# A layer on one Trainium2 core: the dilated attention's mixing split over two steps and fetched back by GpSimd, the next pair's inputs loaded in parts

## The chip, the cores and the metric

The kernel runs on one of the eight cores of one Trainium2 chip. A core has five engines, each with its own instruction queue that it works off in order: TensorE (PE; its weight loads are listed as PEld), VectorE (DVE), ScalarE (ACT), GpSimd (POOL) and SyncE (SP, which here only starts transfers). Transfers can be started from the queues of SP, ACT and GpSimd. The metric is the time of one execution on the device in microseconds (us); lower is better. An engine that reaches an instruction whose inputs are not there, or whose buffer is not free, stands still, and everything behind it in its queue stands too.

## What is computed

One encoder layer on a sequence of 2048 tokens of width 1024, all in 32-bit floats. The part that matters here is the second mixer, the dilated attention of eight heads of 64. It is computed three times, with dilations 1, 4 and 16, and the three results are mixed for each token and head by their log-denominators:

```python
for window, dil in ((128, 1), (512, 4), (2048, 16)):
    half = window // (2 * dil)
    # tokens of the same residue modulo dil form one sequence of 2048 / dil
    o, lse = banded_attention(sub(q), sub(k), sub(v), bias, half, half, None)
    outs.append(o); lses.append(lse)
w = softmax(stack(lses), axis=0)
o = sum(w[..., None] * stack(outs), axis=0)
```

Before it come an RMS norm, the projections to q, k and v of both mixers, and a windowed attention; behind it an output projection with norm and residual, a large feed-forward part with norms, and a gate over a projected side input. The tolerance asks for nearly full 32-bit products, so a large product is made of three matmuls on values split into a high and a low part (`split`: ACT rounds the high part, DVE subtracts it).

## The kernel before

The layer runs in stages: projections, group a (the windowed attention), **group b** (the dilated attention), stage c (the second half of the output projection, norms and transposes), the feed-forward part, the gate. The order of the instructions on every engine is the order in which the program text issues them; there is no planner in the stages from group a on. The work is laid out by hand in steps:

- `Pipe.step` is one step of group b. An item (`b_item`) is one half of a 512-token bank of one pair of heads for one dilation `p`; it has four parts. In step t the step issues `scores` and `probs` of item t, `values` of item t - 3 and `turn` of item t - 2, then calls `feed_b`, then `tick`. There are 96 items: for each of four pairs of heads, the dilations in the order p = 2 (16), 0 (1), 1 (4), eight items each. Items of p = 2 have half as much work as the others.
- `scores` (L806) are matmuls into two buffers of the three of `ps_s`. `probs` (L819, L822) reduces them on DVE (row minimum into `tm`) and takes the exponential on ACT (row sums into `dn`). `turn` transposes on PE into `pt` (two buffers, `ps_t`) and DVE copies to `et`. `values` multiplies with `v` into `po` (one buffer), and every second item ACT evicts `po` to `ops_` (L856, L859, L861).
- `later(dt, fn)` puts a call into the `tick` of the step dt steps on; `tick` comes last in a step.
- `feed_b` first advances every running mixing by one `yield`, then lets `wo_first` go one piece on, in three steps of four from step 12 on (the fourth, t modulo 4 = 3, has none), and from step 86 on `ple`. `wo_first` is the first half of the output projection: six matmuls into `psm` to a piece, four pieces to a tile. The last piece of a tile evicts `psm` (`sgt`, L950), and splits the next tile `o` (`oh_`, `ol_`, L128 and L129, then a square on ACT and sums on GpSimd, L659 to L661); the first piece of the next tile contains the matmul `pss` (L666) on these sums and starts the load of the tile after (L653).
- `mix(pair, ...)` mixes the three results of one pair. It is started by `turn` of the pair's last item, two steps into the next pair's p = 2 items, and takes part in the step in which it starts. Its parts up to the next `yield`: (1) for the row minima and then for the row sums (`kind` 0 and 1): three transposes on PE into one `px`, three copies on ACT (L877, L879, L881), two small writes to DRAM (`sd`, L882, L884, issued by ACT), and then the two loads `sv` (L887), which bring these sums back in token order, from SP; (2) nothing; (3) `mn` and `wt` on DVE (L891 to L894) and an exponential on ACT; (4) five DVE operations, product, sums, reciprocal and the weights `wt` (L898 to L904); (5) the high part `ch` of the weights on ACT (L908, `wr` in the profile); (6) the low part `cl` on DVE (L910); then eight row blocks. A row block has four matmuls `cps` (L917) in two `ps_s` buffers, two DVE products (L920) and two sums on GpSimd (L923, L924); after every second the result goes to DRAM (`obd`, L927). For pairs 0 to 2 the yields stand after blocks 0, 1, 3, 5 and 7, for pair 3 after each.
- The next pair's inputs are loaded by SP when the buffer's last reader has been issued: q after the scores of the last p = 2 item, k with the first p = 0 item, `v` of each dilation after the values of its last item. q, k and `v` for p = 2 are one transfer of 1 MB each; `v` for p = 0 is two (of 256 and 960 KB), `v` for p = 1 is eight of 256 KB, all eight issued in one step.
- The small tiles `text` (biases, L414), `o` (L653) and others share two buffers, `raws`. A load into one of them waits on SP for its last reader, and what follows on SP waits with it.
- After the last item a closing loop advances the last mixing, with two pieces of `ple` in each pass; in its eleventh pass (`loops == 10`) it puts the loads (`c_load`, L1026) and splits (`c_split`) for stage c on the clock, and stage c starts four ticks after that or when the loop ends, whichever is later.

Of the kernel before, what the change touches and what calls it, by code (L numbers as in the profile page):

```python
# [59 lines left out]
def layer(ctx, tc, a, out):  # L60
    nc = tc.nc
    pe, act, dve, pool, sp = nc.tensor, nc.scalar, nc.vector, nc.gpsimd, nc.sync
# [18 lines left out]
    qkd = [dram.tile([128, S], F32, name=f"qkd{i}") for i in range(13)]  # L81
    vad = dram.tile([S, 128], F32, name="vad")
    vb3 = dram.tile([16, 128, 512], F32, name="vb3")
    vb1a = dram.tile([4, 128, 512], F32, name="vb1a")
    vb1o = dram.tile([15, 128, 512], F32, name="vb1o")
# [26 lines left out]
    def row_ap(v, off, ap):  # L112
        return bass.AP(tensor=v.tensor, offset=v.offset + off, ap=ap)
# [121 lines left out]
    def natural(dst, src, half, eng):  # L235
        eng(dst.rearrange("p (a r) -> p a r", r=R)[:, :, 8 * half : 8 * half + 8], src.rearrange("p (r a) -> p a r", r=8))
# [7 lines left out]
    with ExitStack() as st:  # L244
        pst = st.enter_context(tc.tile_pool(name="pst", bufs=3, space=PSUM, reuse_waits="tile"))
        psm = st.enter_context(tc.tile_pool(name="psm", bufs=5, space=PSUM, reuse_waits="tile"))
        with ExitStack() as st1:
# [27 lines left out]
            for tb in range(4):  # L275
                for n in range(4):
                    if tb == 0 and n < 3:
                        c, pl = ((VA0, w1), (0, wcp), (128, wcp))[n]
# [82 lines left out]
    vps = {2: bpre}  # L361
    kps = [bpre, None]

    def load_q(pair):
        q = bpre.tile([128, S], F32, name="bq", tag="bq")
        sp.dma_start(q, qkd[5 + pair])
        return q

    def load_k(pair):
        k = kps[pair % 2].tile([128, S], F32, name="bk", tag="bk")  # L370
        sp.dma_start(k, qkd[9 + pair])
        return k

    VROW, VCHUNK = 512, 128 * 512

# [8 lines left out]
                         row_ap(vb3, (4 + 8 * c) * VROW, [[VCHUNK, 16], [1, n]]))  # L384
            yield

    def load_v(pair, p):
        c0 = 128 * pair
        cols = slice(c0, c0 + 128)
        v = vps[p].tile([128, (19, 32, 16)[p], 128], F32, name=f"v{p}", tag=f"v{p}")  # L390
        if p == 2:
            sp.dma_start(v, vb3[:, :, cols].rearrange("c p n -> p c n"))
        elif p == 0:
            sp.dma_start(v[:, 0:4, :], vb1a[:, :, cols].rearrange("c p n -> p c n"))
            sp.dma_start(v[:, 4:19, :], vb1o[:, :, cols].rearrange("c p n -> p c n"))
        else:
            for b4 in range(4):
                for n, a0 in ((0, 0), (16, 16)):
                    m = 15 if n and b4 == 3 else 16
                    sp.dma_start(v[32 * b4 : 32 * b4 + 32, n : n + m, :],  # L400
                                 row_ap(vb3, 4 * b4 * VCHUNK + a0 * VROW + c0, [[VROW, 32], [32 * VROW, m], [1, 128]]))
        return v

    def load_b3(pair):
# [14 lines left out]
    def later(dt, fn):  # L419
        todo.setdefault(clock[0] + dt, []).append(fn)  # L420
# [64 lines left out]
    st_b = {}  # L485
# [208 lines left out]
    def load_wo_first(to):  # L694
        def part(k):
            halves = load_wo_k(*((wcp, "wc", 2) if k < 2 else (wop, f"wo{k}", 1)), k)
            later(4, lambda: to.append(halves()))

        for k, dt in enumerate((0, 0, 4, 5)):
            later(dt, lambda k=k: part(k))  # L700
# [6 lines left out]
    with ExitStack() as st:  # L707
# [50 lines left out]
        def b_item(pair, p, bank, half):  # L758
# [26 lines left out]
            def scores():  # L785
                if first_ and p == 2:
                    if pair == 0:
                        st_b["v"][0, 0] = load_v(0, 0)
                        st_b["b"][0, 0] = load_bias(0, 1, st_b["text"])
                        later(2, lambda: load_wo_first(st_b["wa"]))  # L790
                        later(10, lambda: st_b["b"].update({(0, 1): load_bias(0, 2)}))
                        later(12, lambda: st_b["v"].update({(0, 1): load_v(0, 1)}))
                        later(18, load_sel)
                    st_b["tm"] = [bp.tile([128, 32], F32, name=f"tm{i}", tag=f"tm{i}", bufs=2) for i in range(3)]
                    st_b["dn"] = [bp.tile([128, 32], F32, name=f"dn{i}", tag=f"dn{i}", bufs=2) for i in range(3)]
                    st_b["qn"] = bm.tile([128, S], F32, name="qn", tag="qn")
                    for hf in range(2):
                        natural(st_b["qn"], st_b["q"][:, hf * S // 2 : (hf + 1) * S // 2], hf, pool.tensor_copy)
                if first_ and p == 0 and pair < 3:
                    st_b["k"][pair + 1] = load_k(pair + 1)  # L800
                box.update(q=st_b["q"], qn=st_b["qn"], k=st_b["k"][pair], vt=st_b["v"][pair, p], tm=st_b["tm"], dn=st_b["dn"])
                ps = box["ps"] = [ps_s.tile([128, 512], F32, name="ps_s", tag="ps_s") for _ in range(2)]
                box["at"] = [place(2 * half + jj) for jj in range(2)]
                for jj, (lq, rk, var, vc) in enumerate(box["at"]):
                    for hh in range(2):
                        pe.matmul(ps[hh][:, 256 * jj : 256 * jj + w], lq[HH[hh]], rk[HH[hh]], start=True, stop=True)  # L806
                if last_ and p == 2 and pair < 3:
                    st_b["q"] = load_q(pair + 1)

            def probs():  # L810
                e = box["e"] = ep.tile([128, 2, 512], F32, name="e", tag="e")
# [29 lines left out]
            def values():  # L841
                if half == 0:
                    st_b["po"] = ps_o.tile([128, 512], F32, name="po", tag="po")
                po = st_b["po"]
                for jj, (lq, rk, var, vc) in enumerate(box["at"]):
                    j = 2 * half + jj
                    for c in range(nch):
                        s0 = 128 * (nch * jj + c)
                        for hh in range(2):
                            pe.matmul(po[HH[hh], 128 * j : 128 * j + 128], vc[c][:, HH[hh]],  # L850
                                      box["et"][hh][:, s0 : s0 + 128], start=c == 0, stop=c == nch - 1)
                if half == 1:
                    opt = ops_[:, op_of(pair, p)]
                    if p == 0:
                        ov = views(opt, 0)[:, :, 32 * bank : 32 * bank + 32].rearrange("p r (j a) -> p r j a", j=4)
                        act.activation(ov, po.rearrange("p (j a r) -> p r j a", j=4, r=R), AF.Copy)  # L856
                    elif p == 1:
                        ov = views(opt, 1)[:, :, bank, :].rearrange("p b (m a) -> p b m a", m=4)
                        act.activation(ov, po.rearrange("p (m a b) -> p b m a", m=4, b=4), AF.Copy)  # L859
                    else:  # L860
                        act.activation(opt[:, 512 * bank : 512 * bank + 512], po, AF.Copy)  # L861
                if last_ and pair < 3:
                    st_b["v"][pair + 1, p] = load_v(pair + 1, p)

            return scores, probs, turn, values

        def mix(pair, tms, dns):
            sd = dram.tile([4, 32, 128], F32, name=f"sd{pair}")
            sv = xp.tile([32, 2, 3, 128], F32, name="sv", tag="sv")
            lo_ = min(op_of(pair, p) for p in range(3))  # L870
            s0, s2 = 1 - lo_, op_of(pair, 2) - lo_
            for kind, srcs in enumerate((tms, dns)):
                px = ps_t.tile([32, 3, 128], F32, name="px", tag="pt")
                for p in range(3):
# [8 lines left out]
                             tr[:, 0, :].rearrange("n (r a) -> n r a", r=R))  # L883
                act.dma_start(row_ap(sd, (2 * kind + 1) * 4096, [[32, 32], [1024, 4], [1, 32]]),  # L884
                             tr[:, 1, :].rearrange("n (b a) -> n b a", b=4))
            for kind in range(2):
                sp.dma_start(sv[:, kind, s0 : s0 + 2, :], sd[2 * kind : 2 * kind + 2].rearrange("k p a -> p k a"))  # L887
            yield
            yield
            mn = xp.tile([32, 128], F32, name="mn", tag="mn")  # L890
# [13 lines left out]
            dve.tensor_mul(wt, wt, rz.unsqueeze(1).to_broadcast([32, 3, 128]))  # L904
            wr = xp.tile([32, 2, 3, 128], F32R, name="wr", tag="sv")
            ch, cl = wr[:, 0], wr[:, 1]
            yield
            act.activation(ch, wt, AF.Copy)  # L908
            yield
            dve.tensor_sub(cl, wt, ch.bitcast(F32))  # L910
# [2 lines left out]
            for n, rr in enumerate(order):  # L913
                for r in (2 * rr, 2 * rr + 1):
                    ps = ps_s.tile([128, 512], F32, name="cps", tag="ps_s")
                    for c, st_, sp_ in ((ch, True, False), (cl, False, True)):
                        pe.matmul(ps[:, 0:384], sel[:, 128 * r : 128 * r + 128], c.rearrange("n k a -> n (k a)"),  # L917
                                  start=st_, stop=sp_)
                    ov = ops_[:, lo_ : lo_ + 3, 128 * r : 128 * r + 128]
                    dve.tensor_tensor(ov, ov, ps[:, 0:384].rearrange("p (k n) -> p k n", k=3), op=ALU.mult)  # L920
                hs = slice(256 * rr, 256 * rr + 256)
                om = oms[rr // 2][:, 256 * (rr % 2) : 256 * (rr % 2) + 256]
                pool.tensor_tensor(om, ops_[:, lo_, hs], ops_[:, lo_ + 1, hs], op=ALU.add)  # L923
                pool.tensor_tensor(om, om, ops_[:, lo_ + 2, hs], op=ALU.add)  # L924
                if n % 2 == 1:
                    qt = rr // 2
                    later(2, lambda qt=qt: sp.dma_start(obd[qt][128 * pair : 128 * pair + 128, :], oms[qt]))  # L927
                if n not in (2, 4, 6) or pair == 3:
                    yield
        def wo_first():  # L930
            wa = st_b["wa"]
# [124 lines left out]
        while mixers:  # L1056
# [3 lines left out]
            if loops == 10:  # L1060
                schedule_c(4)
                start = clock[0] + 4
# [353 lines left out]
    for s in range(E_):  # L1416
        n, hf = s // 2, s % 2
# [243 lines left out]
```

## Time and profile before

| | |
|---|---|
| median of 3 runs | 2747.43 us (2746.08 to 2748.78) |
| the profiled execution | 2751.77 us |
| its span, first to last instruction | 2750.0 us |
| granted TensorE clock, mean | 0.994 |
| PE busy / DVE / ACT / GpSimd | 97% / 64% / 46% / 34% |
| transfers | 324.40 MB, 118 GB/s on average |
| group b in the span | about 590 to 1090 us |

All times of single instructions are from the one profiled execution. A row of the timeline gives the start and the duration in us, the engine, the line of the kernel, the operation, what it writes and reads, how many were merged, and in brackets the idle time of the engine just before, with the instruction or transfer that ended it. "SPq" and "ACTq" are the issue of a transfer by that engine. The clock column is the TensorE clock that was granted, 1.00 being full speed; at 0.50 a matmul takes about twice as long. A row of the list of transfers ends with the KB of one and the median time from its issue to its landing.

### The profile page before, as it was taken

To read this page: it belongs to the slowest core of one execution; us is meant where nothing else is said; L and a number is where in the kernel's file an instruction comes from. 1 tells how busy PE (TensorE), PEld (TensorE's weight loads), DVE (VectorE), ACT (ScalarE), POOL (GpSimd) and SP (SyncE) were. 2 spreads that over 40 slices of the span, in tenths; PEclk is the share of its full clock that TensorE was granted. 3 is DMA by queue.
4 is the path that set the end of the run, shared out by engine and by line. 5 is a ranking of instruction groups with operands and counts; after the bars stand their busy time and mean duration, and the time that the engine had idled before them with its cause. 6 is when DMAs were issued, how large, how long until landed. Compare 5 with 4: busy or idle time off the path is not lost.

```text
span 2750.0 us, 38984 instructions
## 1 busy us (share of the span) xinstructions
PE 2679.0 (97%) x13952; PEld 2127.2 (77%) x13952; DVE 1759.4 (64%) x3423; ACT 1270.6 (46%) x2947; POOL 931.2 (34%) x950
## 2 busy tenths in 40 slices
PE   7999999989999999999999999999999999999998
PEld 6878877767677677877888888888888888887887
DVE  4210245556666653877778777776777778786675
ACT  5321356666565564565444434435444444443422
POOL 3000034432222302544534435435445345344130
PEclk9999999999999999999999999999999999999999
DMA  6232233434543336862212222235222223324553
GB/s 179 77 124 80 97 112 110 159 112 101 135 116 100 78 99 213 277 222 88 83 62 66 81 66 65 77 119 206 98 76 100 92 70 119 104 91 174 181 204 106
DMA packets 248097, 324.40 MB, mean 118 GB/s; under 512 B 20128, under 2 KB 175776, under 8 KB 245504
## 3 DMA queue, kind: packets, MB, share of 16 engines
q1 hardware_dynamic: 220768, 281.73, 32.4%
q10 hardware_dynamic: 27136, 40.18, 4.0%
q8 instruction: 110, 1.80, 0.3%
q14 instruction: 83, 0.68, 0.1%
HBM read 227.16 MB, written 102.04 MB: 120 GB/s over the span
## 4 chain that ended last, share of the span: by engine, by line
PE 52%; DVE 2%; ACT 1%; DMA 1%; issue 1%; POOL 0%; DVEq 0%; POOLq 0%; SPq 0%; ACTq 0%
PE psd L1346 13%; PE psy L1346 10%; PE psu L175 9%; PE psu L173 8%; PE psu L174 8%; PE psm L139 1%; PE psm L138 1%; PE psm L137 1%; DVE y L1617 0%; PE pst L146 0%; DVE dnl L1185 0%; DVE al L1185 0%; DMA out_dram<-y 0%; ACT dmp L1394 0%; DVE y L1600 0%
## 5 line engine op out<-in xcount | busy, mean ns | idle before, releaser
L1355 DVE TENSOR_TENSOR acc<-acc,psd 128x512 f32<-128x512 f32 x488 | 332.5, 685 | 189.1 <-PE psd L1346 183.5
L175 PE MATMUL psu<-vt,upl 128*128 128x512 f32 x1024 | 407.0, 397 | 0.0
L173 PE MATMUL psu<-vt,uph 128*128 128x512 f32 x1024 | 404.9, 395 | 0.0
L174 PE MATMUL psu<-vt,uph 128*128 128x512 f32 x1024 | 400.8, 391 | 0.0
L1190 POOL TENSOR_TENSOR tmp<-rl 128x512 f32<-128x512 f32 x64 | 84.2, 1316 | 668.2 <-ACT rl L1334 668.2
L822 ACT ACTIVATE e<-e,tm 128x256 f32<-128x256 f32 (+1 forms) x384 | 176.5, 461 | 113.6 <-DVE tm L819 113.6
L173 PEld LDWEIGHTS psu<-vt,uph 128*128 128x128 f32 x1024 | 192.5, 188 | 46.3
L175 PEld LDWEIGHTS psu<-vt,upl 128*128 128x128 f32 x1024 | 192.5, 188 | 45.4
L174 PEld LDWEIGHTS psu<-vt,uph 128*128 128x128 f32 x1024 | 192.4, 188 | 45.2
L1355 DVE TENSOR_TENSOR acc<-acc,psy 128x512 f32<-128x512 f32 x248 | 170.1, 686 | 84.1 <-PE psy L1346 73.4
L1333 ACT ACTIVATE rl<-psu 128x512 f32<-128x512 f32 x128 | 76.3, 596 | 303.2 <-PE psu L175 303.0
L1353 POOL TENSOR_TENSOR acc<-acc,dmp 128x512 f32<-128x512 f32 x128 | 191.3, 1506 | 58.4 <-DVE al L1185 31.6
L1346 PE MATMUL psd<-dnl,ah 128*128 128x512 f32 x512 | 203.2, 397 | 0.0
L1346 PE MATMUL psd<-dnh,al 128*128 128x512 f32 x512 | 202.4, 395 | 0.0
L1346 PE MATMUL psd<-dnh,ah 128*128 128x512 f32 x512 | 202.0, 395 | 0.0
L173 PE MATMUL psm<-uhi,wc 128*128 128x512 f32 x448 | 181.6, 410 | 1.0 <-ACT sgt L230 0.7
L175 PE MATMUL psm<-uhi,wc 128*128 128x512 f32 x448 | 178.3, 398 | 0.0
L174 PE MATMUL psm<-ulo,wc 128*128 128x512 f32 x448 | 178.1, 397 | 0.0
L819 DVE CUSTOM_DVE_ANT_0 e<-ps_s,b 128x256 f32<-128x256 f32 (+1 forms) x384 | 122.8, 375 | 74.0 <-PE ps_s L806 73.0
L1346 PE MATMUL psy<-dnh,ah 128*128 128x512 f32 x384 | 151.6, 395 | 4.4 <-ACT dmp L1352 2.8
L1346 PE MATMUL psy<-dnl,ah 128*128 128x512 f32 x384 | 152.4, 397 | 0.0
L1346 PE MATMUL psy<-dnh,al 128*128 128x512 f32 x384 | 151.7, 395 | 0.0
(701 smaller groups left out, 6127.6 us busy)
## 6 DMA issues: line engine op xcount, KB each, us to landing
upraw<-in_w_up_dram SPq DMA_DIRECT2D x64, 512.0 KB, 4.8
dnraw<-in_w_down_dram SPq DMA_DIRECT2D x64, 512.0 KB, 5.3
h<-hd SPq DMA_DIRECT2D x35, 512.0 KB, 4.8
xt<-in_x_dram SPq DMA_DIRECT2D x32, 512.0 KB, 4.6
wraw<-in_w_in_dram SPq DMA_DIRECT2D x26, 512.0 KB, 4.5
qkd<-sgt ACTq DMA_DIRECT2D x52, 256.0 KB, 2.5
mad<-sgt ACTq DMA_DIRECT2D x32, 256.0 KB, 2.1
acc<-mad SPq DMA_DIRECT2D x16, 512.0 KB, 7.5
```

What stands on the lines that cost most here:

```text
L137: pe.matmul(ps, lh(k), rh(k), start=k == 0, stop=False)
L138: pe.matmul(ps, lh(k), rl(k), start=False, stop=False)
L173: pe.matmul(ps, lh(k), rh(k), start=k == 0, stop=False)
L174: pe.matmul(ps, lh(k), rl(k), start=False, stop=False)
L175: pe.matmul(ps, ll(k), rh(k), start=False, stop=k == n - 1)
L819: dve.tensor_tensor_reduce(ej, box["ps"][hh][:, 256 * jj : 256 * jj + w], bs[hh] if p == 2 else bs[hh][:, var], scale=1.0, scalar=3.0e38, ...
L822: act.activation(ej, ej, AF.Exp, bias=tm, scale=-1.0, accum_out=box["dn"][p][:, i : i + 1])
L1190: pool.tensor_tensor(t, x, y, op=op)
L1333: act.activation(rl, ps, AF.Relu)
L1346: pe.matmul(ps, l[:, js], r, start=start and m == 0, stop=m == 2, skip_group_check=True)
L1353: pool.tensor_tensor(t, t, d, op=ALU.add)
L1355: dve.tensor_add(t, t, ps)
```

## The change

The loads of the sums leave SP for GpSimd's queue, and each stands behind the writes of its own kind, with a `yield` after each kind. So the first part takes two steps (minima, then sums), and the minimum `mn` follows in the fifth part instead of the third. For pairs 0 to 2 the `yield` between the weights `wt` and their high part `ch` is gone, and row blocks 0 and 1 share one step, so that the mixing ends in the same step as before. For pair 3 these two yields stay, and it ends two steps later. The loads of q, k and `v` are cut into parts (four for q, k and `v` of p = 2, one and three for p = 0, eight as before for p = 1); those of pair 0 are issued at once as before, those of later pairs by `later`, one part to a step.

```diff
-    def load_q(pair):
+    def load_q(pair, now=True):
         q = bpre.tile([128, S], F32, name="bq", tag="bq")
-        sp.dma_start(q, qkd[5 + pair])
+        in_parts(now, [lambda i=i: sp.dma_start(q[:, i * 512 : i * 512 + 512], qkd[5 + pair][:, i * 512 : i * 512 + 512])
+                       for i in range(4)])
         return q
...
+    def in_parts(now, starts):
+        for i, start in enumerate(starts):
+            if now:
+                start()
+            else:
+                later(i, start)
...
-    def load_v(pair, p):
+    def load_v(pair, p, now=True):
...
         if p == 2:
-            sp.dma_start(v, vb3[:, :, cols].rearrange("c p n -> p c n"))
+            starts = [lambda i=i: sp.dma_start(v[:, 4 * i : 4 * i + 4], vb3[4 * i : 4 * i + 4, :, cols].rearrange("c p n -> p c n"))
+                      for i in range(4)]
         elif p == 0:
-            sp.dma_start(v[:, 0:4, :], vb1a[:, :, cols].rearrange("c p n -> p c n"))
-            sp.dma_start(v[:, 4:19, :], vb1o[:, :, cols].rearrange("c p n -> p c n"))
+            starts = [lambda: sp.dma_start(v[:, 0:4, :], vb1a[:, :, cols].rearrange("c p n -> p c n"))]
+            starts += [lambda i=i: sp.dma_start(v[:, 4 + 5 * i : 9 + 5 * i, :],
+                                                vb1o[5 * i : 5 * i + 5, :, cols].rearrange("c p n -> p c n")) for i in range(3)]
         else:
...
+            starts = [lambda b4=b4, n=n: start(b4, n, n) for b4 in range(4) for n in (0, 16)]
+        in_parts(now, starts)
         return v
...
-                    st_b["k"][pair + 1] = load_k(pair + 1)
+                    st_b["k"][pair + 1] = load_k(pair + 1, False)
...
-                    st_b["q"] = load_q(pair + 1)
+                    st_b["q"] = load_q(pair + 1, False)
...
-                    st_b["v"][pair + 1, p] = load_v(pair + 1, p)
+                    st_b["v"][pair + 1, p] = load_v(pair + 1, p, False)
...
                 act.dma_start(row_ap(sd, (2 * kind + 1) * 4096, [[32, 32], [1024, 4], [1, 32]]),
                              tr[:, 1, :].rearrange("n (b a) -> n b a", b=4))
-            for kind in range(2):
-                sp.dma_start(sv[:, kind, s0 : s0 + 2, :], sd[2 * kind : 2 * kind + 2].rearrange("k p a -> p k a"))
+                pool.dma_start(sv[:, kind, s0 : s0 + 2, :], sd[2 * kind : 2 * kind + 2].rearrange("k p a -> p k a"))
+                yield
             yield
             yield
...
-            yield
+            if pair == 3:
+                yield
             act.activation(ch, wt, AF.Copy)
...
-                if n not in (2, 4, 6) or pair == 3:
+                if n % 2 == 1 or pair == 3:
                     yield
```

`load_k` is changed as `load_q` is; the function `start` for p = 1 holds the one transfer that stood in the loop before.

More of the change, by code (lines that the diff above doesn't have):

```diff
@@ L362, in layer, with load_k @@
     kps = [bpre, None]
-    def load_q(pair):
+    def load_q(pair, now=True):
         q = bpre.tile([128, S], F32, name="bq", tag="bq")
-        sp.dma_start(q, qkd[5 + pair])
+        in_parts(now, [lambda i=i: sp.dma_start(q[:, i * 512 : i * 512 + 512], qkd[5 + pair][:, i * 512 : i * 512 + 512])
+                       for i in range(4)])
         return q
-    def load_k(pair):
+    def load_k(pair, now=True):
         k = kps[pair % 2].tile([128, S], F32, name="bk", tag="bk")
-        sp.dma_start(k, qkd[9 + pair])
-        return k
+        in_parts(now, [lambda i=i: sp.dma_start(k[:, i * 512 : i * 512 + 512], qkd[9 + pair][:, i * 512 : i * 512 + 512])
+                       for i in range(4)])
+        return k
+    def in_parts(now, starts):
[4 more added lines that the diff above has]
+                later(i, start)
     VROW, VCHUNK = 512, 128 * 512
@@ L391, in load_v, with start @@
         if p == 2:
-            sp.dma_start(v, vb3[:, :, cols].rearrange("c p n -> p c n"))
+            starts = [lambda i=i: sp.dma_start(v[:, 4 * i : 4 * i + 4], vb3[4 * i : 4 * i + 4, :, cols].rearrange("c p n -> p c n"))
+                      for i in range(4)]
         elif p == 0:
-            sp.dma_start(v[:, 0:4, :], vb1a[:, :, cols].rearrange("c p n -> p c n"))
-            sp.dma_start(v[:, 4:19, :], vb1o[:, :, cols].rearrange("c p n -> p c n"))
-        else:
[L397 to L401, printed above, removed]
+            starts = [lambda: sp.dma_start(v[:, 0:4, :], vb1a[:, :, cols].rearrange("c p n -> p c n"))]
+            starts += [lambda i=i: sp.dma_start(v[:, 4 + 5 * i : 9 + 5 * i, :],
+                                                vb1o[5 * i : 5 * i + 5, :, cols].rearrange("c p n -> p c n")) for i in range(3)]
+        else:
+            def start(b4, n, a0):
+                m = 15 if n and b4 == 3 else 16
+                sp.dma_start(v[32 * b4 : 32 * b4 + 32, n : n + m, :],
+                             row_ap(vb3, 4 * b4 * VCHUNK + a0 * VROW + c0, [[VROW, 32], [32 * VROW, m], [1, 128]]))
+            starts = [lambda b4=b4, n=n: start(b4, n, n) for b4 in range(4) for n in (0, 16)]
+        in_parts(now, starts)
         return v
```

## Prediction

> **What bounds the kernel now.** I read the page first, then busy time by stretch, then the timeline of each engine where the change works.
>
> ```profile
> span 2750.0 us, 38984 instructions
> ...
> PE 2679.0 (97%) x13952; PEld 2127.2 (77%) x13952; DVE 1759.4 (64%) x3423; ACT 1270.6 (46%) x2947; POOL 931.2 (34%) x950
> ```
>
> TensorE (PE) is busy for 97% of the span, so a change that leaves its work alone can only take away its gaps and the stretches in which its clock was granted at half. The change touches the stage from 590 to 1090 us (group b). Stretches of that stage, in the order PE, PEld, DVE, ACT, POOL, clock, DMA share, GB/s:
>
> ```profile
> 590.00:1090.00 500.00, 469.25 (x3481) 354.30 (x3482) 306.42 (x1117) 293.28 (x975) 116.51 (x169) 0.97 0.44 124
> ...
> 683.00:740.00 57.00, 50.37 (x344) 35.74 (x345) 35.34 (x139) 28.84 (x107) 18.58 (x28) 0.94 0.57 147
> 606.90:613.30 6.40, 6.40 (x32) 4.09 (x34) 3.63 (x17) 3.76 (x16) 0.00 (x0) 0.50 0.97 373
> 712.40:719.20 6.80, 6.80 (x27) 5.10 (x26) 3.24 (x12) 2.56 (x9) 2.35 (x4) 0.50 0.55 190
> 923.70:927.20 3.50, 3.50 (x17) 2.78 (x18) 3.00 (x12) 2.24 (x10) 0.00 (x0) 0.54 1.21 188
> ```
>
> PE idles 500 - 469.25 = 30.8 us in the stage; the mixing of pair 0 (683 to 740) holds 57 - 50.37 = 6.6 us of it. To this come the stretches at half clock: 6.80 us at 0.50 in the mixing of pair 0 (3.4 us lost), 3.5 us at 0.54 in that of pair 2 (1.6 us lost). The change reaches only a part of these 36 us, and 0.2% of the time, about what a measurement of this kernel can tell from no change, is 5.5 us.
>
> The waits of PE in the mixings (timeline; in brackets the idle time and what ended it). I call the step in which a mixing begins s0, the next s1.
>
> ```profile
> 688.50 0.50 PE L173 MATMUL psm<-wo,oh__6596 128*128 128x512 f32 x1 [0.70 <-ACT oh__6596 L128]
> 691.24 0.38 PE L666 MATMUL pss<-ones,o 128*128 128x1 f32 x2 [0.82 <-POOL o L661]
> 697.84 0.71 PE L806 MATMUL ps_s<-bk,bq 64*128 64x128 f32 x6 [0.73 <-DVE tm L819]
> 699.99 0.66 PE L850 MATMUL po<-et,v 128*64 128x128 f32 x8 [1.44 <-DVE z L901]
> 709.81 0.62 PE L917 MATMUL cps<-wr,sel 32*128 32x384 f32 x2 [1.58 <-DVE tm L819]
> 711.36 1.13 PE L806 MATMUL ps_s<-bk,qn 64*128 64x256 f32 x6 [0.30 <-DVE ops L920]
> ...
> 810.15 0.66 PE L850 MATMUL po<-et,v 128*64 128x128 f32 x8 [0.47 <-ACT ops L861]
> 811.77 0.50 PE L173 MATMUL psm<-wo,oh__7981 128*128 128x512 f32 x1 [0.38 <-ACT oh__7981 L128]
> ...
> 921.55 0.71 PE L806 MATMUL ps_s<-bk,bq 64*128 64x128 f32 x6 [0.41 <-DVE tm L819]
> 923.70 0.87 PE L850 MATMUL po<-et,v 128*64 128x128 f32 x8 [1.44 <-DVE z L901]
> 934.07 0.62 PE L917 MATMUL cps<-wr,sel 32*128 32x384 f32 x2 [0.59 <-DVE tm L819]
> 935.62 1.13 PE L806 MATMUL ps_s<-bk,qn 64*128 64x256 f32 x6 [0.30 <-DVE ops L920]
> ...
> 1041.11 0.49 PE L139 MATMUL psm<-pw,ol__10404 128*128 128x512 f32 x1 [1.68 <-DVE ol__10404 L129]
> ```
>
> **Where they come from.** Pair 0, other engines:
>
> ```profile
> 691.66 0.52 SPq L414 DMA_DIRECT2D text<-sk  x1
> 692.28 1.00 SPq L887 DMA_DIRECT2D sv<-sd  x2
> 693.33 6.34 SPq L400 DMA_DIRECT2D v<-vb  x8
> 695.58 0.56 DVE L891 TENSOR_TENSOR mn<-sv 32x128 f32<-32x128 f32 x1 [1.56 <-DMA sv<-sd]
> 699.77 1.14 SPq L653 DMA_DIRECT2D o<-oad  x1
> 707.98 0.63 ACT L128 ACTIVATE oh__6828<-o 128x512 fp32r<-128x512 f32 x1 [1.38 <-DMA o<-oad]
> ```
>
> The two `sv` loads stand on SP behind a `text` load that waited for its buffer, so DVE waits 1.56 us at `mn`, and PE 0.73 and 1.44 us after it. (The second row names DVE `z`; PE really waits for ACT's eviction of `po`, whose exponentials came late.) The eight `v` loads hold SP for 6.34 us; `o` starts behind them, ACT waits 1.38 us for it, and PE 1.58 us for what DVE does after that.
>
> **Part 1: the `sv` loads go to GpSimd, and `mn` stands two steps later (s4 instead of s2).** This removes 0.73 + 1.44 = 2.17 us in pair 0 and 0.41 + 1.44 = 1.85 in pair 2. In pair 1 no load was late, but the sums fell in the step of `oh_`: moved, they free 0.47 + 0.38 = 0.85. Each pair pays a second wait of PE for a `px` buffer. In pair 1 I take 0.35, what the first costs now (the row is quoted below). In pairs 0 and 2 step s1 has `oh_` as well: ACT is freed of three copies and two DMA issues in s0, so 0.70 + 0.82 go, but the second `px` waits behind about the same chain (`ol_`, four reductions, one `et`): zero, between a loss of 0.35 (one `px` wait) and a gain of 0.82 (the longer of the two).
>
> The price of a load issued by GpSimd is in no row. From below it is SP's: 0.5 us to issue (1.00 for two), 1.7 to land. From above I let the issue last as long as the whole wait behind SP did, 1.56 us more, the nearest row with `sv` in it; I take the lower end, as the transfer is the same. What queues behind it on GpSimd is `o` (L660), `ro` and the copies of `text`; `o` in s0 comes after `oh_` (ready at 688.50), and the first `sd` writes have landed by then (683.07, 1.5 us for ACT, 2.2 to land: 686.8), so that wait is covered.
>
> ```profile
> sd<-tr ACTq DMA_DIRECT2D x16, 16.0 KB, 2.2
> sv<-sd SPq DMA_DIRECT2D x8, 32.0 KB, 1.7
> 683.07 0.50 PE L875 MATMUL px<-ident,tm 128*32 128x128 f32 x3 [0.35 <-DVE et L836]
> ```
>
> The last `sd` write of s1 should be issued near 691.5 (an estimate: 3 us after PE's matmuls of s1 begin) and land at 693.7; the load ends at 693.7 + 0.5 + 1.7 = 695.9, or 697.5 by the upper end. `mn` comes up on DVE near 699 (PE's row of 699.99, 2.17 earlier, is s4 at 697.8; its reductions and `et` come first), so 1.5 to 3.1 us are spare. The two later steps, 4 us or more, would cover the 1.56 us without GpSimd too; its queue by itself may bring nothing.
>
> **Part 2: fewer steps.** For pairs 0 to 2 the step between `wt` and `ch` (`wr` in the rows) goes, so five DVE operations, ACT's `wr` and, in pairs 0 and 2, the next tile's `sgt`, `oh_` and `ol_` all fall in s5. The rows that price it:
>
> ```profile
> 698.80 0.53 DVE L898 TENSOR_TENSOR sv<-wt,sv 32x384 f32<-32x384 f32 x1
> 700.97 0.55 DVE L904 TENSOR_TENSOR wt<-wt,rz 32x384 f32<-32x384 f32 x1
> 703.32 0.51 ACT L908 ACTIVATE wr<-wt 32x384 fp32r<-32x384 f32 x1
> 704.22 0.49 PE L173 MATMUL psm<-wo,oh__6596 128*128 128x512 f32 x1
> 705.80 0.72 PE L806 MATMUL ps_s<-bk,bq 64*128 64x128 f32 x8
> 705.91 0.69 ACT L950 ACTIVATE sgt<-psm,ro 128x512 f32<-128x512 f32 x1
> 707.62 0.61 PE L917 MATMUL cps<-wr,sel 32*128 32x384 f32 x2
> 708.64 0.69 DVE L129 TENSOR_TENSOR ol__6829<-o,oh__6828 128x512 fp32r<-128x512 f32 x1 [3.15 <-ACT oh__6828 L128]
> ...
> L836 DVE COPY et<-pt 128x256 f32<-128x256 f32 x12 | 4.5, 414 | 0.1
> ```
>
> Take PE 2.17 us earlier than now. Its transposes of s5 end at 704.22 - 2.17 = 702.05; two `et` copies of 0.41 take DVE to 702.8; the five operations last 701.52 - 698.80 = 2.72, to 705.5; then ACT `wr` 0.51, `sgt` 0.69, a DMA issue 0.4 (SP's took 0.5), `oh_` 0.63 (the row of 707.98), to 707.8; `ol_` 0.69, to 708.5; PE went on 0.5 after `ol_` in the old trace (709.33 to 709.81), so 709.0. PE has finished s5 at 705.80 - 2.17 = 703.6, does s6 in 1.82 (705.80 to 707.62) and two matmuls of s7 in 0.4 (six take 1.13), and stands at 705.8. A stall of **3.2 us**, in pairs 0 and 2. What goes there is 1.58 + 0.30 and 0.59 + 0.30, since row block 0 leaves s6; with two blocks in s7 I add 0.3, the shortest of the waits that such blocks show above. Pair 1 splits no tile in s5: no stall.
>
> **Part 3: q, k and v in parts.** The same bytes, 11 more issues for a pair, of 0.8 us at most (6.34 for eight), on SP. The last part of `v` for p = 1 goes out in s8 and is read in s18, the others have longer; ten steps of 2 us at least (s6 above) hide the delay; if that cover were gone, 6.34 us of issues would show. The gain is that `o` is no longer late; that is in the 1.58 already.
>
> **Part 4: pair 3 and the end.** Its mixing ends two steps later. Each has two pieces of `ple` for PE, which now run ahead of the row blocks instead of behind them, so work is only reordered. The five DVE operations move away from the last `wo` splits; I take the 1.68 as won, less 0.35 for `px`: 1.3, between -0.35 and 1.7.
>
> ```profile
> o<-obd SPq DMA_DIRECT2D x16, 256.0 KB, 4.0
> ```
>
> The loads of the next stage start in the eleventh pass of the closing loop, which now makes two passes more, so loads and splits fall one step earlier against that stage's matmuls. I cost that at nothing: they must wait for the same buffers as now. If the first came too late instead, one landing of 4.0 us would show.
>
> **Sum.** Pair 0: 2.17 + 1.88 - 3.2 - 0.3 = 0.55. Pair 2: 1.85 + 0.89 - 3.2 - 0.3 = -0.75. Pair 1: 0.85 - 0.35 = 0.5. End: 1.3. Clock: 3.4 + 1.6 = 5.0 us lost now; each stall of 3.2 us should bring its own low stretch, between the shortest and the longest above (3.5 and 6.80 us: 1.6 to 3.4 lost), 2.5 each: zero. In all 1.6 us won. The profiled execution took 2751.77 us (1.77 around its span), 4.3 above the median of the three runs; its differences carry over: 2747.4 - 1.6, some **2745.5 us**.
>
> **The rivals.** *No new stall* (0.18): if ACT or DVE gets through s5 sooner, the 6.4 us and the low clock go too: 1.6 + 6.4 + 5.0 = 13.0 won, 2734.4 us. For it speaks that PE, delayed anywhere in s5, hides it; against it, this row, where PE waited for DVE behind two `wo` splits of ACT and DVE in the same way, with half clock from 606.90 on:
>
> ```profile
> 606.62 2.07 PE L806 MATMUL ps_s<-bk,qn 64*128 64x256 f32 x6 [2.10 <-DVE tm L819]
> ```
>
> *A stall without the low clock* (0.17): 1.6 + 5.0 = 6.6 won, 2740.8 us. For it: 0.59 us of wait at 934.07 brought no low clock. Against it: 2.10 and 1.58 did. [...]
>
> *The GpSimd load is late* (0.10, slower): from 3.1 us over SP's price on, DVE waits at `mn` again, and PE pays 2.17/1.56 = 1.4 us for each. With 3 us too late in three pairs: 12.6 lost, less 1.6: 2758 us. Against it stands the spare time above. [...]
>
> The forecast keeps 0.55, with a range of its own from 2742 to 2750. Faster 0.35, same 0.55, slower 0.10. For 8 in 10 the range reaches down past the second rival and part of the first, 2737, and up to 2751.
>
> **What would show it.** Right: no wait at `mn`; a PE wait of 2 to 4 us for DVE `tm` in s7 of pairs 0 and 2 behind `ol_`, then clock 0.50; ACT's wait for `o` gone. Wrong: `mn` waiting for `sv`, or gaps of PE in the three mixings under 2 us each.

## The result, and the profile after

The changed kernel takes 2766.79 us (median of 4 runs, 2764.06 to 2771.6) beside 2746.76 us for the kernel before: ratio 1.0067, 95% interval 1.0054 to 1.0079, 20 us slower by the medians and 18 by the ratio. The forecast was 2745.5, and the range ended at 2751. The profiled execution took 2767.07 us. The head of its page:

```profile
span 2765.3 us, 39074 instructions
```

The span is 2765.3 - 2750.0 = 15.3 us longer; the rest of the 20 is that the profiled execution of before lay some 5 us above its median. Where it was lost shows at instructions that both kernels have. The small matmuls `pss` of stage c are good marks: one group, with its first and last start. Rows of the groups of instructions (ns min/median/max, then first and last start), of the kernel before, then of the one after:

```profile
L1040 PEld LDWEIGHTS pss<-ones,o x64: 188/192/193, 1087.9 to 1197.5; 128*128 128x128 f32 x64
```

```profile
L1054 PEld LDWEIGHTS pss<-ones,o x64: 187/192/192, 1090.1 to 1214.9; 128*128 128x128 f32 x64
```

At the first mark the changed kernel is 1090.1 - 1087.9 = 2.2 us late, at the last 17.4; the rest of the span gives 2.1 back. **The loss lies in stage c, which the diff does not touch**: 124.8 us from mark to mark instead of 109.6. What PE waits for there (list of waits: us in total, times, longest; 1088 to 1216 us), before and after:

```profile
PE pst L1157 <- DVE vt L1161: 1.0, 2, 0.6
PE pst L1157 <- DVE acc L1151: 1.0, 1, 1.0
PE pst L1157 <- DVE mso L1042: 0.5, 1, 0.5
```

```profile
PE pst L1171 <- DVE mso L1056: 9.2, 7, 1.8
PE psd L137 <- DVE mso L1056: 2.8, 1, 2.8
PE psd L137 <- DVE acc L1146: 1.7, 2, 1.1
PE psm L137 <- ACT pst L1009: 1.0, 1, 1.0
```

2.5 us have become 14.7. The 9.2 us in seven places come from the early split. One of the seven in the changed kernel, and a place of the same kind in the kernel before:

```profile
1135.41 0.63 ACT L128 ACTIVATE oh__11265<-o 128x512 fp32r<-128x512 f32 x1 [0.87 <-PE psd L138]
1136.08 0.69 DVE L129 TENSOR_TENSOR ol__11266<-o,oh__11265 128x512 fp32r<-128x512 f32 x1 [1.47 <-ACT oh__11265 L128]
1140.83 0.14 DVE L1056 TENSOR_SCALAR mso<-pss 128x1 f32<-128x1 f32 x1
1141.05 0.63 PE L1171 MATMUL pst<-ident,acc 128*128 128x128 f32 x4 [1.80 <-DVE mso L1056]
```

```profile
1129.44 0.15 DVE L1042 TENSOR_SCALAR mso<-pss 128x1 f32<-128x1 f32 x1
1129.50 0.68 DVE L129 TENSOR_TENSOR ol__11261<-o,oh__11260 128x512 fp32r<-128x512 f32 x1
1129.58 0.66 PE L1157 MATMUL pst<-ident,acc 128*128 128x128 f32 x4 [0.50 <-DVE mso L1042]
```

In the first four rows ACT stands at a split `oh_` (0.87 us) until PE has read the old contents of that buffer, DVE stands at `ol_` behind it (1.47 us), and all that DVE has queued behind `ol_` (the norms, evictions of `psd`, `mso`) comes late, so PE waits in its turn (1.80 us). That is a ring: PE's reading sets ACT free, ACT DVE, DVE PE. In the kernel before `ol_` stands behind `mso`, and DVE does not wait at it.

The 2.8 us at `psd` have another cause, the early load:

```profile
1090.95 0.37 SPq L1040 DMA_DIRECT2D o<-obd  x1
1092.96 0.99 SPq L1132 DMA_DIRECT2D acc<-mad  x2
1101.67 0.75 DVE L1146 SCALAR_TENSOR_TENSOR acc<-psd,ro,acc 128x512 f32<-128x512 f32 x1 [4.04 <-DMA acc<-mad]
1102.34 0.15 DVE L1056 TENSOR_SCALAR mso<-pss 128x1 f32<-128x1 f32 x1
1102.47 0.50 PE L137 MATMUL psd<-wo,oh__10861 128*128 128x512 f32 x1 [2.79 <-DVE mso L1056]
```

SP stood at the load of `o` for 11.3 us, until its buffer was free at the first `pss`; two loads of 512 KB (`gb`, `gm`) and the first `mad` stood behind it, and DVE waited 4.04 us for `mad`. In the kernel before, `gb` and `gm` went out at 1080.83 and 1081.47, and `mad` right behind `o`. Half clock followed this wait, 1.7 us lost (1102 to 1108 us). So by this trace the larger part of the loss in stage c is the split's, and some 4.5 us are the load's.

Group b came out nearly as forecast in its places. PE's rows in the mixings of pairs 0 and 2 with the long waits, and the stretch of half clock behind each (PE, PEld, DVE, ACT, POOL, clock, DMA share, GB/s):

```profile
678.62 0.50 PE L888 MATMUL px<-ident,tm 128*32 128x128 f32 x3 [0.35 <-DVE et L849]
685.04 0.50 PE L888 MATMUL px<-ident,dn 128*32 128x128 f32 x3 [2.29 <-DVE et L849]
703.73 1.99 PE L819 MATMUL ps_s<-bk,qn 64*128 64x256 f32 x6 [2.73 <-DVE tm L832]
...
911.31 0.50 PE L888 MATMUL px<-ident,dn 128*32 128x128 f32 x3 [2.60 <-DVE et L849]
931.54 1.13 PE L819 MATMUL ps_s<-bk,qn 64*128 64x256 f32 x6 [2.73 <-DVE tm L832]
```

```profile
702.00:716.00 14.00, 12.27 (x54) 9.12 (x54) 8.29 (x32) 5.77 (x22) 4.83 (x7) 0.63 0.82 201
932.00:944.00 12.00, 12.00 (x55) 8.77 (x52) 6.88 (x25) 4.61 (x20) 4.70 (x7) 0.57 0.06 23
```

### The profile page after: what moved, and what is told of

It reads as the page before. It is cut to its first block, busy times and chain, and to the rows that moved or that the text cites. A ratio compares the mean times of both kernels' runs of the same rounds, so it can differ in the third digit from the quotient of the medians.

```text
span 2765.3 us, 39074 instructions
## 1 busy us (share of the span) xinstructions
PE 2685.7 (97%) x13952; PEld 2130.1 (77%) x13952; DVE 1762.8 (64%) x3423; ACT 1274.0 (46%) x2947; POOL 944.1 (34%) x958
## 4 chain that ended last, share of the span: by engine, by line
PE 51%; DVE 2%; DMA 1%; ACT 1%; issue 0%; POOL 0%; DVEq 0%; POOLq 0%; ACTq 0%; SPq 0%
PE psd L1360 13%; PE psy L1360 10%; PE psu L175 9%; PE psu L173 8%; PE psu L174 8%; PE psm L139 1%; PE psm L138 1%; PE psm L137 1%; DVE y L1631 0%; PE pst L146 0%; DVE dnl L1199 0%; DMA out_dram<-y 0%; ACT dmp L1408 0%; DVE y L1614 0%; DVE y L1630 0%
```

## The experiments

**The theory.** In the closing loop the loads and splits of stage c are put on the clock in pass 10. The last mixing now needs two passes more. Before, the loop ended one tick ahead of the start of stage c; now it ends one tick after it. So every load and split is due one step earlier against the matmuls of stage c. There are two `oh_` buffers, and a tile of stage c takes two steps of PE: a split one step early asks for the buffer that the half issued in that very step still reads. The main rival: GpSimd's queue and the new stalls of group b, seen late. The "first kernel" in the text ahead of a result is that of experiment 1 in number 5, and of experiment 9 in number 11.

Each kernel was timed in five rounds or more beside the kernel before on the same chip; those chips were a little slower (the kernel before had medians of 2750.55 to 2751.8 on them), so the ratios are what to compare. One thousandth is 2.75 us.

**1. The changed kernel with the plan moved.**

```diff
-            if loops == 10:
+            if loops == 12:
```

> The changed kernel with one number changed: the loads and splits of stage c are put on the plan two passes of the closing loop later (pass 12 instead of 10), so that they stand against that stage's matmuls as in the kernel before. Theory A (the shifted plan of stage c costs the time): stage c takes again what it took before, some 15 us less than in the changed kernel; group b stays at about +1 us; 2745 to 2751 us, and the wait of ACT for PE at the split of stage c (25.0 us in 13 places) falls to about 9 in 4. Rival B (the cost sits in group b: GpSimd's queue, the new stalls of PE and the half clock after them, seen late only because PE and the loads drift): still 2762 to 2770 us.

2761.6 us, ratio 1.0038 (1.0026 to 1.005): about 8 us under the changed kernel, between the two theories and nearer to the rival. The trace says why it is not all. Stage c's ring is gone, and something else stands at its start (marks, then PE's waits from 1088 to 1216, then a stretch with its clock):

```profile
L1054 PEld LDWEIGHTS pss<-ones,o x64: 187/192/338, 1093.6 to 1206.2; 128*128 128x128 f32 x64
```

```profile
PE pss L1054 <- POOL o L1048: 3.9, 1, 3.9
PE pst L1171 <- DVE mso L1056: 0.6, 1, 0.6
```

```profile
1092.00:1102.00 10.00, 8.41 (x25) 6.86 (x26) 1.60 (x4) 1.26 (x2) 2.41 (x3) 0.66 0.77 256
```

Stage c takes 112.6 us from mark to mark, 12.2 less than 124.8; but PE reaches the first `pss` before GpSimd has its sums, waits 3.9 us and then loses 10 * (1 - 0.66) = 3.4 us of clock.

**2. The shift alone, in the kernel before.**

```diff
-            if loops == 10:
+            if loops == 9:
                 schedule_c(4)
-                start = clock[0] + 4
+                start = clock[0] + 5
```

> The kernel before with the shift alone: loads and splits of stage c go on the plan in pass 9 instead of 10 and the stage still begins where it did, one step later against them. Nothing of the change is in it. Theory A: stage c is longer by 12 to 18 us, 2758 to 2766 us, with ACT's waits for PE at the split of stage c near 25 us in a dozen places. Rival B: nothing there depends on one step, 2745 to 2750 us.

2763.27 us, ratio 1.0041 (1.0029 to 1.0053): 11 us slower with no part of the change in it. Marks and PE's waits:

```profile
L1040 PEld LDWEIGHTS pss<-ones,o x64: 186/192/192, 1090.0 to 1212.4; 128*128 128x128 f32 x64
```

```profile
PE pst L1157 <- DVE mso L1042: 9.1, 7, 1.8
PE psd L137 <- DVE mso L1042: 1.1, 1, 1.1
```

122.4 us, and the first wait of PE is that of the changed kernel (9.1 in 7 places, 9.2 in 7 there): the theory holds from this side too.

**3. Only the splits later.**

```diff
-                later(lead + 2 * n - 2, lambda n=n: c_split(n))
+                later(lead + 2 * n - 1, lambda n=n: c_split(n))
```

> The changed kernel, where only the splits of stage c are due one step later (where they stood in the kernel before); the loads of o stay one step early. Theory A1 (the early split takes an oh_ buffer that PE still reads; ACT waits and DVE's work behind it is late): nearly all comes back, 2747 to 2753 us. Theory A2 (the early load waits on SP for its buffer, and mad, gb and gm behind it come late): little comes back, 2761 to 2767 us.

2756.6 us, ratio 1.0016 (1.0006 to 1.0025), 14 us under the changed kernel. The time is a little above A1's band and clear of A2's. SP's waits for the early loads are as long as there, and PE waits 0.6 us at `psd` instead of 2.8. Marks; PE's waits; SP's longest:

```profile
L1054 PEld LDWEIGHTS pss<-ones,o x64: 186/192/192, 1094.4 to 1206.3; 128*128 128x128 f32 x64
```

```profile
PE pss L1054 <- POOL o L1048: 2.5, 1, 2.5
PE pst L1171 <- DVE mso L1056: 1.5, 3, 0.5
PE psd L137 <- DVE acc L1146: 0.6, 1, 0.6
```

```profile
SPq L1040 <- PE pss L1054: 52.0, 13, 11.3
```

111.9 us: it is in the main the split (A1 over A2). The first `pss` waits here too, so PE reaches `psd` later, which may hide a part of the load's price; a kernel with only the loads put back was not tried.

**4. The plan made in pass 11**: aligned with stage c like pass 12, but a pass earlier against the last row blocks.

> The changed kernel with the plan of stage c made in pass 11 of the closing loop: loads and splits stand against stage c's matmuls as in the kernel before and as with pass 12, but one pass earlier against the end of the mixing. With pass 12 the ratio to the kernel before was 1.0038, and PE waited 3.91 us at the first matmul of stage c for GpSimd's o, with clock 0.67 in the ten us after. Theory E (ple's pieces, taken two in each of two more passes, no longer stand behind the last row blocks, and it is they that hid the first split): a pass more of lead covers it again, 3.9 and some 3 of clock come back, ratio 1.000 to 1.002. Rival F (the wait is set by ACT's order, the split stands behind the same evictions however early it is planned): 1.003 to 1.005.

2755.38 us, ratio 1.0016 (1.0007 to 1.0025). Stage c 111.2 us (1091.8 to 1203.0), and the wait at its first `pss` is 2.5 us instead of 3.9: theory E, though one pass does not cover it all. With two more passes the loop uses up four more pieces of `ple`, which in the kernel before stood behind the last row blocks. That they hid the first split is argued from the order; experiment 6, with one pass more than before, fits it, as no such wait is left there.

**5. The two parts of the merged step apart again**, in the aligned kernel of experiment 1, by giving the step between `wt` and `ch` back to pairs 0 to 2:

```diff
-            if pair == 3:
-                yield
+            yield
             act.activation(ch, wt, AF.Copy)
```

> As the first kernel of this call, and the step between wt and ch is back for pairs 0 to 2 as well, so that the five operations of DVE and the next tile's split fall in two steps. Theory C (the merged step makes the stalls of PE at the scores of s7, 2.73 us in pairs 0 and 2, and each brings half clock for some 9 us, 4.5 lost): both go, 2 * (2.7 + 4.5) = 14 us under the first kernel, 2732 to 2738 us. Rival D (with the step back the old waits of PE at the row blocks, 1.58 and 0.59 us, and their low clock come back): within 4 us of the first kernel, 2743 to 2750 us.

2741.18 us, ratio 0.9964 (0.9952 to 0.9975), 20 us under experiment 1. In this order the last row blocks of pairs 0 to 2 fall in s11, after the next pair's first result for p = 0 has been written over a part of what they mix: other values, the same work, so this order is a probe and not a kernel to use. The gain is larger than theory C's 14 us, and the time still lies above its band, which was set under the 2745 to 2751 us hoped for in experiment 1. In the merged step's place PE waits 0.53 us for `tm`, not 2.73, and no half clock follows:

```profile
703.50 1.13 PE L819 MATMUL ps_s<-bk,qn 64*128 64x256 f32 x6 [0.53 <-DVE tm L832]
```

```profile
702.00:716.00 14.00, 13.21 (x91) 9.28 (x89) 10.80 (x47) 9.27 (x34) 4.63 (x7) 1.00 0.83 222
```

**6. The same within the length of a mixing**: the step is back, and one of the two empty steps ahead of `mn` goes (`mn` in s3). Pair 3 then needs one pass less, and pass 10 is right for the plan.

> The changed kernel with the step between wt and ch back for every pair, and one of the two empty steps ahead of mn taken out for it, so that a mixing is as long as in the changed kernel (pairs 0 to 2) and all values are those of the reference; pair 3 has one pass less, which sets the plan of stage c right without an edit. Theory C (the merged step makes two stalls of 2.73 us and the half clock after them): these go, the second of three runs of group b's 16 us is seen again, ratio 0.995 to 0.998. Rival G (mn one step earlier comes up before GpSimd's load has landed; in the changed kernel the second sv load is issued at 689.2 and mn starts at 694.4, a step is about 3 us): mn waits, PE stands after it with half clock, ratio 0.999 to 1.002.

2748.77 us, ratio 0.999 (0.998 to 1.0). Stage c begins at 1084.7 and takes 109.6 us, as before the change, with no wait at its first `pss`. PE's waits in pair 0:

```profile
685.87 0.50 PE L888 MATMUL px<-ident,dn 128*32 128x128 f32 x3 [1.48 <-DVE et L849]
700.53 0.66 PE L863 MATMUL po<-et,v 128*64 128x128 f32 x8 [0.48 <-ACT ops L874]
703.71 1.13 PE L819 MATMUL ps_s<-bk,qn 64*128 64x256 f32 x6 [1.30 <-DVE tm L832]
```

```profile
702.00:716.00 14.00, 12.57 (x62) 9.21 (x60) 9.58 (x39) 7.28 (x27) 4.81 (x7) 0.76 0.81 218
```

Theory C in kind, but 1.30 us are left at the same place and still bring half clock (0.76 from 702 to 716 us), so the gain falls short of its band. The ratio lies in rival G's band, but its reason is out: `mn` does not wait.

**7. As 6, with the `sv` loads on SP.**

> As the kernel with two steps, but the sv loads go back to SP's queue. Theory H (the later mn covers the load whoever starts it, GpSimd's queue brings nothing): within 3 us of that kernel. Rival J (on SP they wait again behind text and the parts of v): DVE waits 1 to 2 us at mn and PE 1.4 times that in pairs 0 and 2, with half clock: 4 to 12 us more than that kernel.

2748.63 us, ratio 0.9993 (0.9984 to 1.0002): the same. GpSimd's queue by itself brings nothing here; the later `mn` covers the load.

**8. As 6, with q, k and `v` loaded whole.**

> As the kernel with two steps, but q, k and v are loaded whole as in the kernel before. Theory K (the parts keep SP free for o, and let pair 0 begin earlier): ACT waits again 1.4 us for o in pair 0, PE 1.58 and 0.59 with half clock in pairs 0 and 2, some 5 us, and up to 4.4 us are lost before pair 0's mixing: 5 to 10 us more than that kernel. Rival L (o has slack, the parts bring nothing): within 2 us of it.

2755.11 us, ratio 1.0022 (1.0011 to 1.0032), above experiment 6 by 0.0032 or 9 us (6.3 by the medians), as theory K has it. `o` is late in pairs 0 and 2 (rows of PE and ACT):

```profile
706.36 0.63 ACT L128 ACTIVATE oh__6827<-o 128x512 fp32r<-128x512 f32 x1 [1.90 <-DMA o<-oad]
708.19 1.35 PE L806 MATMUL ps_s<-bk,qn 64*128 64x256 f32 x6 [2.79 <-DVE tm L819]
...
937.20 0.63 ACT L128 ACTIVATE oh__9304<-o 128x512 fp32r<-128x512 f32 x1 [3.38 <-DMA o<-oad]
939.03 2.07 PE L806 MATMUL ps_s<-bk,qn 64*128 64x256 f32 x6 [4.27 <-DVE tm L819]
```

**9. As 6, with both kinds of sums in s0 again** (three empty yields behind them, so that `mn` stays in s3).

> As the kernel with two steps (0.999 of the kernel before, with PE's waits at the second px of 1.48, 0.30 and 2.45 us), but both kinds of sums are turned in one step s0 as in the kernel before, three steps ahead of mn; the sv loads stay with GpSimd. Theory M (the second px, behind ol_, four reductions and one et, costs more than the crowding of ACT in s0 did): the waits of 1.5 and 2.5 us and the half clock of pair 2 go, 0.82 to 1.5 come back at oh_ and pss of s1: 3 to 7 us under the kernel with two steps, ratio 0.9965 to 0.998. Rival N (ACT's three more copies and two DMA issues in s0 delay oh_ as they did before): no gain, 0.9985 to 1.0005.

2749.51 us, ratio 0.9991 (0.998 to 1.0002). The waits at the second `px` go, 0.79 and 0.81 us come back at `oh_` and `pss` of s1 in pair 0: no gain that shows, rival N.

**10. The parts alone, in the kernel before.**

> The kernel before with the loads of q, k and v in parts, and nothing else of the change. Theory K (the parts are worth some 9 us, as leaving them out of the kernel with two steps cost 2755.11 - 2748.77 = 6.3 in the medians): o and sv come in time, the waits of 1.38 us of ACT for o and 1.58 and 0.59 of PE go: ratio 0.9970 to 0.9985. Rival O (the parts only help where mn was moved, or bring nothing): 0.9995 to 1.001.

2748.36 us, ratio 0.9991 (0.9983 to 1.0): at most 4.7 us, and none is not excluded; between the two theories. PE's wait at the row block of pair 0 fell from 1.58 to 0.60 us. A second thing shows: `mn` now waits 0.86 us for `sv` instead of 1.56, and PE's wait at `po` is still 1.44 (rows of DVE and PE):

```profile
692.25 0.65 DVE L904 TENSOR_TENSOR mn<-sv 32x128 f32<-32x128 f32 x1 [0.86 <-DMA sv<-sd]
...
697.09 0.66 PE L863 MATMUL po<-et,v 128*64 128x128 f32 x8 [1.44 <-DVE z L914]
707.41 0.61 PE L930 MATMUL cps<-wr,sel 32*128 32x384 f32 x2 [0.60 <-DVE tm L832]
```

**11. As 9, with the `sv` loads on SP.**

> As the first kernel of this call, with the sv loads on SP. Theory H (with parts and a later mn the queue of GpSimd brings nothing): within 3 us of it. Rival J: the loads stand behind text and parts of v, mn waits 1 to 2 us, 4 us or more above it.

2744.76 us, ratio **0.9976 (0.9965 to 0.9986)**: faster than both kernels, by 0.24% and, through the ratios to the kernel before, 0.9% (0.9976 / 1.0067). Against experiment 9 it is 0.0015 lower, outside theory H's 3 us to the good side, but the intervals overlap a little. Its trace has no shorter waits in the mixings (1.29 us at the row blocks of pairs 0 and 2 in both), so the source of this part is not shown; what is shown is that the loads need not leave SP. Of the change it keeps the parts, a later `mn`, and row blocks two to a step.

**12. As 11, with `wt` and `ch` merged again for pairs 0 to 2**, now in s4, where no tile is split.

> As the kernel with the sums in one step and the sv loads on SP (0.9976 of the kernel before), but for pairs 0 to 2 the step between wt and ch is taken out again, as in the change; as mn stands one step earlier than in the changed kernel, the merged step is now s4 and not s5, in which the next wo tile is split. Theory P (the stall of 2.73 us comes from the collision of the five DVE operations, ACT's wr and the split in one step): no wait of PE for tm over 1.5 us in pairs 0 and 2, ratio 0.9965 to 0.9985. Rival Q (the merged step stalls PE wherever it stands, by the length of its own chain through DVE and ACT): waits of 2 us or more with half clock again, ratio 0.9995 to 1.003.

2746.83 us, ratio 0.9988 (0.9977 to 0.9998). PE's waits near the merged step of pair 0:

```profile
701.82 0.66 PE L863 MATMUL po<-et,v 128*64 128x128 f32 x8 [0.56 <-ACT ops L874]
704.57 1.26 PE L930 MATMUL cps<-wr,sel 32*128 32x384 f32 x4 [0.97 <-DVE tm L832]
```

No stall of 2.7: it took the collision with the split (theory P). Half clock followed in pair 0 all the same (0.50 from 706 to 718 us), which rival Q had named. The time is a little above P's band, and its interval overlaps that of experiment 11.

## Why the prediction was wrong

- **Part 4 is the step that failed**: "loads and splits fall one step earlier against that stage's matmuls. I cost that at nothing: they must wait for the same buffers as now." The premise is right and the price is wrong: that they wait for the same buffers is the cost. ACT reaches the split a step sooner, stands there for PE, and holds DVE with it; SP does the same at the load of `o`, with `mad` behind it. Experiment 2 gives the shift alone as 11 us; in the two traces stage c is longer by 12.8 us (122.4 - 109.6) there and by 15.2 in the changed kernel; experiments 3 and 4 take 14 us of the loss away. The forecast asked what a late load would cost (one landing of 4.0 us) and not what an early split or load costs; that DVE's wait for `mad` came to 4.04 us is chance, as it is another load.
- **Part 4, the two passes**: "work is only reordered" was wrong as well. The pieces of `ple` that ran ahead were the cover of the first split: 3.9 and 2.5 us at the first `pss` in experiments 1 and 4, with half clock behind (3.4 and 1.7 us lost; argued, as said there). The 1.68 us taken as won stayed: 1.67.

```profile
1048.01 0.50 PE L139 MATMUL psm<-pw,ol__10503 128*128 128x512 f32 x1 [1.67 <-DVE ol__10503 L129]
```

- **Part 1**: the mechanism was right: no wait at `mn`, the 0.73, 1.44, 0.41 and 1.44 us gone. But the second `px`, put at zero in pairs 0 and 2, took 2.29 and 2.60. And the 1.44 us at `po` do not follow the lateness of the load (experiment 10: the same with the load 0.7 us less late); in the later kernels with `mn` in s3 0.36 to 0.56 are left. The load of GpSimd landed 3.0 us after its issue (median of eight), where the prediction took 0.5 and 1.7 together; the two later steps covered that.
- **Part 2**: right in place and nearly in size: 2.73 us for 3.2, in pairs 0 and 2, none in pair 1, behind `ol_`. Experiments 5, 6 and 12 show its cause.
- **The clock** was mis-sized. "Zero, net" became the whole loss of group b. The three mixings and what lies between, 676 to 1018 us, before and after (PE, clock, DMA share, GB/s):

```profile
676.00:1018.00 342.00, 324.66 (x2504) 0.98 0.39 105
```

```profile
676.00:1018.00 342.00, 324.72 (x2460) 0.95 0.39 104
```

  PE idles as long in both (17.3 us); the clock has lost 342 * 0.03 = 10 us more, as each stall of 2.73 us was followed by some 10 us at half, not by 3.5 to 6.8, and one of the new waits at `px` by 3.4. That used up the 4.45 us by which pair 0's mixing began sooner (683.07 - 678.62; the sum had no such term), and 2.2 more by the first mark. The size of this loss varies: with group b as in the kernel before, experiment 2 lost 12.0 us there and that kernel 8.5 (added up in steps of 2 us).
- **Part 3**: right that `o` comes in time, too small in size: in the new order of steps the parts are worth 6 to 9 us (experiment 8), on the old one at most 4.7 (experiment 10).
- **The rivals**: none took place. "No new stall" and "a stall without the low clock" are out by the rows above: two gaps of 2.73 us came, and clock 0.63 (702 to 716 us) and 0.57 (932 to 944 us) behind them. "The GpSimd load is late" is out, as `mn` does not wait in any of the three mixings. What took place, a wait made in a stage that the diff does not name, was not among them. The three signs named for being right were all met (no wait at `mn`; 2.73 us in s7, then clock 0.50; ACT's wait for `o` gone), while the time was 20 us off: all three look at the mixings alone.
- **The sum** ends at 2747.4 - 1.6 = 2745.8; the 2745.5 of the forecast is 0.3 lower, which changes nothing.

## What to carry to other kernels

A plan tied to a count of passes is part of every edit that adds a pass: work out, for each thing on the plan, which engine stands at it and what that engine has queued behind. An instruction issued earlier than its buffer comes free is not free: the splits and loads of stage c, one step early, held up what stood behind them, 11 us in experiment 2. And when steps are merged, look for the other chain that falls into the same step: five DVE operations cost PE 2.73 us beside a split and 1.0 us one step away from it (experiment 12). Signs that would show a forecast right must cover every stage whose order moves, not only the one that the diff is about.

## What the runs showed of the hardware

Gaps of PE could cost more through the clock than by their own length: 1.30 us of wait at 703.71 in experiment 6 was followed by half clock (14 * (1 - 0.76) = 3.4 us lost), 0.53 at 703.50 in experiment 5 was not. The length of the gap alone does not decide it: 0.60 at 707.41 in experiment 10 was followed by some 10 us at half and 0.49 at 818.47 in the changed kernel by the row below, while 0.59 at 934.07 in the kernel before, 1.48 at 685.87 in experiment 6 and 2.29 at 685.04 in the changed kernel were followed by none. The stretches have sizes that look like multiples: a loss of 4 * (1 - 0.59) = 1.6 us in the row below, 14 * 0.37 = 5.2 and 12 * 0.43 = 5.2 in the two rows of the first section, and in the kernel before 6.80 us at 0.50, 3.4 lost. All are near 1.7 us times 1, 2 or 3. Read in steps of 0.2 us, the changed kernel has clock 0.50 from 819.9 to 823.3 and from 912.1 to 915.5 us (3.4 us each), and from 703.8 to 714.1 and 932.5 to 942.8 us (10.3 us each). Added up in steps of 2 us from 676 to 1018 us, the loss is 8.5 us in the kernel before, 18.8 in the changed kernel, 12.0 in experiment 2 and 22.2 in experiment 3: 5, 11, 7 and 13 times 1.71, which the stretch near 840 us lost in the kernel before.

```profile
820.00:824.00 4.00, 4.00 (x21) 2.26 (x21) 0.74 (x5) 0.27 (x1) 1.93 (x3) 0.59 1.13 223
```

What decides whether half clock follows a gap, and how long it then lasts, was not tried. Between profiles of one order the loss varies (676 to 790 us: clock 0.96 in the changed kernel, 0.93 in experiments 3 and 4, whose group b is the same), which is likely part of the scatter of the times.
